# Order of expert-row gathers in a one-layer decoder kernel: value rows ahead of u rows, denser routing steps, one norm moved

## The chip, the cores and the metric

One core of a Trainium2 chip runs the kernel; the other cores are idle. The metric is device time in microseconds (us) for one execution of the whole layer. In the profile PE is TensorE (matmuls), PEld its weight loads, DVE is VectorE, ACT ScalarE, POOL GpSimd, SP SyncE. DMA transfers are issued from SP's queue (SPq), apart from the indirect gathers, which POOL issues.

## The reference, cut to what matters

1024 tokens of width 1024 pass through one decoder layer. The change concerns the last of its sublayers, PEER: each token picks 8 x 16 = 128 of 16384 single-neuron experts (product keys, two top-16 lists per head), and expert e adds g_e v_e gelu(u_e . x).

```python
x   = layer_norm(DN_ALPHA * x + mix, ln1_g, ln1_b)
ple = sigmoid(x @ ple_gate_w) * (p @ ple_proj_w)
ffn = peer(x, peer_wq, peer_subkeys, peer_u, peer_v)
x   = layer_norm(DN_ALPHA * x + ffn + ple, ln2_g, ln2_b)

# peer, for a block of 128 tokens: xb (t, d), ib and gb (t, 128)
u   = jnp.take(u_tab, ib, axis=0)                       # 128 rows of 1024 per token
hid = gelu(einsum("td,ted->te", xb, u))
vv  = jnp.take(v_tab, ib, axis=0)
out = einsum("te,ted->td", gb * hid, vv)
```

## The kernel before, in words

**Tiles and halves.** The 1024 tokens are eight tiles of 128. They go through the mixer and the projections in two halves of four tiles. `post(hf, ...)` takes a half from the mixer's output to the end of the embedding: output projection, first layer norm, queries and scores of eight heads, then the per-layer embedding (four blocks of the gate and projection matmuls). The second half's `post(1, m)` carries the writing of dense gates in its embedding: `dense_gates` (L961 to L990) of two tiles, whose steps stand between the embedding's matmuls.

**Two ways to the experts.** Four tiles, GT = (0, 1, 6, 7), here gathered blocks 0 to 3, fetch their experts' rows. Four, DT = (4, 5, 2, 3), go through all 16384 experts as dense matmuls with a gate matrix that is zero where an expert wasn't picked. The dense part, `dense` (from L992), is the last stage: `hidden` (L1026) computes 128 experts' activations (matmuls named ph), `value` (L1046) multiplies by the value table (matmuls pv) and adds into acc (L1059). At its end the generator of gathers is drained, the two row vectors of the second layer norm are loaded (`norm2`, L951) and four norms are done (`finish`, L1082).

**The gathers.** For a gathered block, `gather_u` (L838) has 128 steps: one indirect DMA on POOL (L844) brings one u row for each of the 128 tokens (a tile of 128 x 1024 float32), and one DVE instruction (L846) multiplies it with x and accumulates. `gather_v` (L854) has 32 rounds: four indirect DMAs (L873), then eight matmuls (L880, 16 records in the trace) that add the four rows' contributions into the PSUM tile ffn. Behind the last round it takes the norm's row vectors (norm2), bt, the statistics and the norm.
The rows of both live in one ring of ROWS = 7 buffers in order of emission, with MORE = 4 more in the dense part. `route` (L741) turns a tile's scores into expert numbers and gates in 29 or 30 steps, nearly all on DVE: 16 selections (`select16`, L730, on the tile sc), eight of the candidates, one of ranks, four of key lookups, and for a gathered tile the transposed index list.

**The order.** `gathers` weaves three generators, us (u rows), routes and vs (value rows): `weave` (L901) takes one step of each in turn, and a step that can't go on yet yields -1. `pump` (L230) runs this generator from within the main work: each matmul group gives credits (at RATE 0.8, 0.6, 1.0, 1.2 by phase), and each step costs its yield (1.46 a row, 0.7 to 2.0 a route step). Phase 2 is `post(1, m)`, phase 3 the dense part. Steps emitted in phase 3 have priority over the dense work (LATER is -10000), and are held (PIN, issue_after) behind the last DVE instruction ahead of the dense part. Value rows of a block need all of its u rows; routes start only when the tile's half is scored (flow["scored"]), and block 3's route only when block 0 is done.

Of the kernel before, what the change touches and what calls it, by code (L numbers as in the profile page):

```python
# [14 lines left out]
ALU = mybir.AluOpType  # L15
# [9 lines left out]
NH = T // HT  # L25
TT = HT // P
# [10 lines left out]
GT = (0, 1, 6, 7)  # L37
DT = (4, 5, 2, 3)
# [29 lines left out]
def kernel(ctx: ExitStack, tc: tile.TileContext, a: dict, out: bass.AP, tap=None):  # L68
    nc = tc.nc
# [65 lines left out]
    def row_bcast(t, src):  # L135
        nc.sync.dma_start(t, bass.AP(tensor=src.tensor, offset=src.offset, ap=[[0, P], [1, D]]))
        return t
# [82 lines left out]
    flow = {"it": None, "credit": 0.0, "rate": 0.0, "scored": 0, "phase": 0, "routing": False}  # L220
# [30 lines left out]
    def row(name):  # L251

        flow["rows"] = flow.get("rows", -1) + 1
        pool = more[0] if more and flow["rows"] % (ROWS + MORE) >= ROWS else gath
        return pool.tile([P, D], F32, name=name, tag="rows")
# [341 lines left out]
    def layer_norm(y, st, g, b, w):  # L597

        mv = small.tile([P, 2], F32, name=f"mv{w}")
        nc.vector.bn_aggr(mv, st)  # L600
        rs = small.tile([P, 1], F32, name=f"rs{w}")
        nc.scalar.activation(rs, mv[:, 1:2], AF.Sqrt, bias=eps_l)
        nc.vector.reciprocal(rs, rs)
        nc.vector.scalar_tensor_tensor(y, y, mv[:, 0:1], g, op0=ALU.subtract, op1=ALU.mult)
        nc.vector.scalar_tensor_tensor(y, y, rs, b, op0=ALU.mult, op1=ALU.add)
# [120 lines left out]
    def drain(it):  # L726
        for _ in it:
            pass

    def select16(v, i, n, s):  # L730
# [5 lines left out]
        nc.vector.max_index(i[:, n, 8:16], v[:, n, 8:16], s)  # L736

    def route(ti, dense, R, lists=None):

        if dense:  # L740
# [97 lines left out]
    def gather_u(ti, idx, idxT, gate, H):  # L838
        x1 = peer.tile([P, D], F32, name="x1g")
        nc.sync.dma_start(x1, x1_d[ti])  # L840
        hid = small.tile([P, NSEL], F32, name="hid")
        for s in range(NSEL):
            ug = row("ug")
            nc.gpsimd.indirect_dma_start(out=ug, out_offset=None, in_=a["peer_u"],  # L844
                                         in_offset=bass.IndirectOffsetOnAxis(ap=idx[:, s:s + 1], axis=0))
            nc.vector.scalar_tensor_tensor(ug, ug, 1.0, x1, op0=ALU.mult, op1=ALU.mult, accum_out=hid[:, s:s + 1])  # L846
            yield 1.46
        if tap:
            tap(f"hid{ti}", hid)
        nc.scalar.activation(hid, hid, AF.Gelu)  # L850
        nc.vector.tensor_mul(hid, hid, gate)
        H.append(hid)

    def gather_v(ti, idx, idxT, gate, H):  # L854
        ffn = ps_f.tile([P, D], F32, name="ffn")
        nc.tensor.transpose(ffn[:, :P], H[0], ident)
        pw = small.tile([P, P], F32, name="pw")
        nc.scalar.activation(pw, ffn[:, :P], AF.Copy)
        N = 4
        for ph in range(32 // N):  # L860

            w32 = peer.tile([P, 4, N, 32], F32, name="w32", bufs=2)
            nc.gpsimd.memset(w32, 0.0)
            for c in range(4):
                dst = w32[:, c].rearrange("p r e -> p (r e)")[:, ph * N:ph * N + (N - 1) * 33 + 1:33]
                nc.scalar.activation(dst, pw[:, 32 * c + ph * N:32 * c + ph * N + N], AF.Copy)
            for r in range(N):

                rows_v = []
                for c in range(4):  # L870
                    t = 32 * c + ph * N + r
                    vg = row("vg")
                    nc.gpsimd.indirect_dma_start(out=vg, out_offset=None, in_=a["peer_v"],  # L873
                                                 in_offset=bass.IndirectOffsetOnAxis(ap=idxT[:, t:t + 1], axis=0))
                    rows_v.append(vg)
                    if c < 3:
                        yield 1.46
                with ExitStack() as side:
                    for n, (e, c) in enumerate((e, c) for e in range(2) for c in (3, 0, 1, 2)):
                        mm = nc.tensor.matmul(ffn[32 * c:32 * c + 32, e * 512:(e + 1) * 512], w32[:, c, r],  # L880
                                              rows_v[c][:, e * 512:(e + 1) * 512], start=ph == 0 and r == 0,
                                              stop=ph == 32 // N - 1 and r == N - 1, skip_group_check=True)
                        if n == 0:

                            side.enter_context(tc.issue_after(mm.ins))
                            side.enter_context(tc.high_priority())
                yield 1.46
        ln2 = norm2()
        bt = row("bt")
        st = small.tile([P, 2, 6], F32, name="st2")  # L890
        nc.sync.dma_start(bt, base_d[ti])
        for e in range(2):
            es = slice(e * 512, (e + 1) * 512)
            nc.vector.scalar_tensor_tensor(bt[:, es], bt[:, es], 0.5, ffn[:, es], op0=ALU.mult, op1=ALU.add)
            nc.vector.bn_stats(st[:, e], bt[:, es])
        finish(ti, bt, st, ln2)

    def weave(*its):

        its = list(its)  # L900
        while its:  # L901
            stuck = True
            for it in list(its):
                x = next(it, None)
                if x is None:
                    its.remove(it)
                elif x >= 0:
                    yield x
                if x is None or x >= 0:
                    stuck = False  # L910
            if stuck:
                yield -1.0

    def gathers():

        H = {t: [] for t in GT}
        done = []

        def routes():
            while at[0] < ROUTE:  # L920
                yield -1.0
            for t in sorted((t for t in range(T // P) if t % TT >= DIRECT[t // TT]), key=lambda t: (t // TT, t in GT)):

                while t in GT and GT.index(t) > 2 and len(done) < GT.index(t) - 2:
                    yield -1.0
                while flow["scored"] <= t // TT:
                    yield -1.0
                flow["routing"] = True
                yield from route(t, t in DT, R)
                flow["routing"] = False  # L930

        at = [0]

        def us():
            for t in GT:
                while t not in R:
                    yield -1.0
                for x in gather_u(t, *R[t], H[t]):
                    at[0] += 1
                    yield x  # L940

        def vs():
            for t in GT:
                while not H[t]:
                    yield -1.0
                yield from gather_v(t, *R[t], H[t])
                done.append(t)

        yield from weave(us(), routes(), vs())

    def norm2():  # L951

        return [row_bcast(row(n), a[n]) for n in ("ln2_g", "ln2_b")]

    def finish(ti, bt, st, ln2):
        layer_norm(bt, st, *ln2, 2)
        nc.sync.dma_start(out[ti * P:(ti + 1) * P], bt)
# [35 lines left out]
    def dense(X):  # L993
        with ExitStack() as dctx:
# [7 lines left out]
            st = [a_p.tile([P, 2, 6], F32, name=f"std{c}") for c in range(TT)]  # L1002
# [74 lines left out]
                W = Wn  # L1077
            if flow["it"] is not None:
                drain(flow["it"])
            ln2 = norm2()  # L1080
            for c in range(TT):
                finish(DT[c], acc[c], st[c], ln2)  # L1082

    R = {}

# [39 lines left out]
    for n in range(2):  # L1125
        nc.sync.dma_start(X[n][:, :, ND * P:].bitcast(F32), xs_d[n])
    flow["rate"], flow["phase"] = RATE[3], 3
    dense(X)


# [54 lines left out]
```

## Time and profile before

| | us |
|---|---|
| median of 3 runs | 3281.31 (3279.74 to 3281.79) |
| profiled execution | 3276.95 |
| its span | 3275.1 |
| its mean granted TensorE clock | 0.958 of full |

| engine | busy us | share of the span |
|---|---|---|
| PE | 3043.4 | 93% |
| PEld | 2320.7 | 71% |
| DVE | 2338.4 | 71% |
| ACT | 1197.7 | 37% |
| POOL | 1177.0 | 36% |

The profile moves 954.45 MB, 291 GB/s on average; the gathers are 536.94 MB of it. Busy times overlap between engines, and a share over the whole span is a mean over stages: the mixers, the second half's `post` with its embedding (about 1400 to 1573 us), the dense part (to about 3232 us) and what follows it. The span stands 1.85 us below the time of its execution.

### The profile page before, as it was taken

Reading aid. Unit: us, or ns where it says so; the run is one execution under the profiler, and the core shown is the slowest. Engines: PE = TensorE matmul, PEld = TensorE weight load, DVE = VectorE, ACT = ScalarE, POOL = GpSimd, SP = SyncE. Lnnn points to the kernel's source line nnn. Section 1 sums busy time; section 2 is a strip of 40 time slices with the busy share of each in tenths; the row PEclk is TensorE's granted clock in tenths of the full one; section 3 lists DMA queues with packets and bytes.
Section 4 is the critical chain, followed back from the end, with each engine's and each line's share of the span. In section 5 each row is a group of like instructions: output and inputs, shape, how many; then the busy total and the mean of one; then the engine's idle time right before and its main releaser. Section 6 shows DMA issues by size and latency. Waiting matters only on the chain.

```text
span 3275.1 us, 48259 instructions
## 1 busy us (share of the span) xinstructions
PE 3043.4 (93%) x17160; PEld 2320.7 (71%) x17160; DVE 2338.4 (71%) x5615; ACT 1197.7 (37%) x2258; POOL 1177.0 (36%) x1066
## 2 busy tenths in 40 slices
PE   8999989787899898877899999999999999999996
PEld 6778777666777686667677777777777777777663
DVE  7656557977789799997888866666676666665333
ACT  6433323262344365566423322222233222223220
POOL 0000000434422345351344544444544445443453
PEclk9999999898999998888999999999999999999997
DMA  4444355787777898998999999999988999998998
GB/s 169 143 169 152 135 186 169 281 301 267 295 274 247 298 357 310 337 313 273 320 346 345 339 330 326 340 335 350 329 325 322 344 334 334 341 328 316 354 320 303
DMA packets 368914, 954.45 MB, mean 291 GB/s; under 512 B 34432, under 2 KB 116480, under 8 KB 364576
## 3 DMA queue, kind: packets, MB, share of 16 engines
q0 software_dynamic: 147456, 536.94, 44.9%
q1 hardware_dynamic: 221216, 414.43, 36.1%
q8 instruction: 135, 2.21, 0.3%
q14 instruction: 107, 0.88, 0.1%
HBM read 862.10 MB, written 89.13 MB: 290 GB/s over the span
## 4 chain that ended last, share of the span: by engine, by line
PE 73%; DVE 13%; DMA 5%; ACT 4%; issue 3%; POOL 1%; SPq 0%; DVEq 0%; POOLq 0%; ACTq 0%
PE ph L263 7%; PE ffn L880 7%; PE ph L265 7%; PE pv L263 7%; PE pv L264 7%; PE ph L264 7%; PE pv L265 7%; DVE ug L846 3%; DMA vg<-in_peer_v_dram,idxT 1%; PE pg L985 1%; DMA ug<-in_peer_u_dram,idx 1%; PE pgr L263 1%; PE pgr L264 1%; PE pgr L265 1%; PE pgb L265 1%
## 5 line engine op out<-in xcount | busy, mean ns | idle before, releaser
L844 POOL DMA_INDIRECT ug<-in_peer_u_dram,idx x512 | 602.9, 1178 | 1417.2 <-DVE idxT L831 598.4
L873 POOL DMA_INDIRECT vg<-in_peer_v_dram,idxT x512 | 555.6, 1085 | 650.0 <-DVE ug L846 291.2
L846 DVE SCALAR_TENSOR_TENSOR ug<-ug,x1g 128x1024 f32<-128x1024 f32 x512 | 619.6, 1219 | 37.6 <-DMA ug<-in_peer_u_dram,idx 35.2
L263 PE MATMUL ph<-x1hl,uh 128*128 128x512 f32 x1024 | 408.4, 399 | 9.7 <-ACT uh L259 9.7
L265 PE MATMUL ph<-x1hl,ul 128*128 128x512 f32 x1024 | 407.3, 398 | 2.2 <-DVE ul L260 2.2
L264 PE MATMUL ph<-x1hl,uh 128*128 128x512 f32 x1024 | 407.5, 398 | 0.0
L264 PE MATMUL pv<-vl,wdh 128*128 128x512 f32 x1024 | 402.9, 394 | 0.0
L265 PE MATMUL pv<-vh,wdl 128*128 128x512 f32 x1024 | 399.9, 392 | 0.0
L263 PE MATMUL pv<-vh,wdh 128*128 128x512 f32 x1024 | 398.0, 394 | 0.0
L259 ACT ACTIVATE uh<-ur 128x512 fp32r<-128x512 f32 x256 | 159.8, 626 | 445.6 <-PE ph L264 430.5
L880 PE MATMUL ffn<-vg,w 128*32 128x512 f32 x2048 | 272.8, 620 | 27.8 <-DMA vg<-in_peer_v_dram,idxT 27.7
L259 ACT ACTIVATE vh<-vr 128x512 fp32r<-128x512 f32 x256 | 160.8, 628 | 359.3 <-PE pv L265 341.1
L260 DVE TENSOR_TENSOR ul<-ur,uh 128x512 fp32r<-128x512 f32 x256 | 175.7, 688 | 153.1 <-ACT uh L259 150.0
L1059 DVE SCALAR_TENSOR_TENSOR acc<-acc,pv 128x512 f32<-128x512 f32 x256 | 167.6, 682 | 129.8 <-PE pv L265 129.7
L260 DVE TENSOR_TENSOR vl<-vr,vh 128x512 fp32r<-128x512 f32 x256 | 176.0, 687 | 111.0 <-ACT vh L259 110.7
L263 PEld LDWEIGHTS ph<-x1hl,uh 128*128 128x128 f32 x1024 | 193.0, 188 | 72.1 <-issue 15.1
L263 PEld LDWEIGHTS pv<-vh,wdh 128*128 128x128 f32 x1024 | 192.1, 188 | 62.4 <-issue 21.0
L264 PEld LDWEIGHTS pv<-vl,wdh 128*128 128x128 f32 x1024 | 192.3, 188 | 61.5 <-issue 19.3
L265 PEld LDWEIGHTS ph<-x1hl,ul 128*128 128x128 f32 x1024 | 192.8, 188 | 59.6 <-issue 9.2
L264 PEld LDWEIGHTS ph<-x1hl,uh 128*128 128x128 f32 x1024 | 192.9, 188 | 55.4 <-issue 10.9
L265 PEld LDWEIGHTS pv<-vh,wdl 128*128 128x128 f32 x1024 | 192.3, 188 | 54.4 <-issue 12.6
L985 PE MATMUL pg<-oi,oj 128*128 128x128 f32 x1024 | 157.9, 297 | 39.0 <-ACT oi L984 15.6
(477 smaller groups left out, 5967.0 us busy)
## 6 DMA issues: line engine op xcount, KB each, us to landing
ur<-in_uT_dram SPq DMA_DIRECT2D x256, 256.0 KB, 6.3
vr<-in_peer_v_dram SPq DMA_DIRECT2D x256, 256.0 KB, 6.5
g_d<-gst SPq DMA_DIRECT2D x32, 1024.0 KB, 12.7
gt<-g_d SPq DMA_DIRECT2D x32, 1024.0 KB, 8.9
raw_zx<-in_w_z_dram SPq DMA_DIRECT2D x16, 512.0 KB, 5.8
raw_zv<-in_w_v_dram SPq DMA_DIRECT2D x16, 512.0 KB, 6.2
raw_zy<-in_w_z_dram SPq DMA_DIRECT2D x16, 512.0 KB, 4.5
raw_ga<-in_w_z_dram SPq DMA_DIRECT2D x16, 512.0 KB, 5.3
```

Of the source, the lines that this page charges most:

```text
L259: nc.scalar.activation(h, src, AF.Copy)
L260: nc.vector.tensor_tensor(l, src, h, op=ALU.subtract)
L263: nc.tensor.matmul(o, wh, xh, start=first, stop=False)
L264: nc.tensor.matmul(o, wh, xl, start=False, stop=False)
L265: nc.tensor.matmul(o, wl, xh, start=False, stop=last)
L844: nc.gpsimd.indirect_dma_start(out=ug, out_offset=None, in_=a["peer_u"], in_offset=bass.IndirectOffsetOnAxis(ap=idx[:, s:s + 1], axis=0))
L846: nc.vector.scalar_tensor_tensor(ug, ug, 1.0, x1, op0=ALU.mult, op1=ALU.mult, accum_out=hid[:, s:s + 1])
L873: nc.gpsimd.indirect_dma_start(out=vg, out_offset=None, in_=a["peer_v"], in_offset=bass.IndirectOffsetOnAxis(ap=idxT[:, t:t + 1], axis=0))
L880: mm = nc.tensor.matmul(ffn[32 * c:32 * c + 32, e * 512:(e + 1) * 512], w32[:, c, r], rows_v[c][:, e * 512:(e + 1) * 512], start=ph == 0 a ...
L985: nc.tensor.matmul(o[:, :, r], oj[:, t], oi, start=True, stop=True)
L1059: nc.vector.scalar_tensor_tensor(acc[c][:, es], acc[c][:, es], 0.5 if g == 0 else 1.0, o[c], op0=ALU.mult, op1=ALU.add)
```

## The change

Three things are altered.

1. In the second half's embedding (phase 2, both halves scored; the new function `embedding`), `weave` no longer takes one step of each generator in turn. It goes through them from the last to the first, vs, routes, us, and stops at the first that gives a step. `routes` doesn't begin a tile there. A route that has already begun goes on only when vs has no step.
2. In the dense part (phase 3) `routes` passes on only every third step of a route, so three of its steps go in one turn of the weave.
3. For the last gathered block, `gather_v` no longer issues its final sum, statistics and norm behind its last round: it loads its norm rows and bt there, and leaves the rest as a function `end` in the list `ends`. The dense part's end takes those same norm rows instead of loading its own pair, does its four norms, and then calls `end`.

```diff
         bt = row("bt")
         st = small.tile([P, 2, 6], F32, name="st2")
         nc.sync.dma_start(bt, base_d[ti])
-        for e in range(2):
-            es = slice(e * 512, (e + 1) * 512)
-            nc.vector.scalar_tensor_tensor(bt[:, es], bt[:, es], 0.5, ffn[:, es], op0=ALU.mult, op1=ALU.add)
-            nc.vector.bn_stats(st[:, e], bt[:, es])
-        finish(ti, bt, st, ln2)
+
+        def end():
+            for e in range(2):
+                es = slice(e * 512, (e + 1) * 512)
+                nc.vector.scalar_tensor_tensor(bt[:, es], bt[:, es], 0.5, ffn[:, es], op0=ALU.mult, op1=ALU.add)
+                nc.vector.bn_stats(st[:, e], bt[:, es])
+            finish(ti, bt, st, ln2)
+
+        if ti == GT[-1]:
+            ends.append((end, ln2))
+        else:
+            end()
+
+    ends = []
+
+    def embedding():
+        return flow["phase"] == 2 and flow["scored"] == NH
 
     def weave(*its):
         its = list(its)
         while its:
             stuck = True
-            for it in list(its):
+            last = embedding()
+            for it in reversed(its) if last else list(its):
                 x = next(it, None)
                 if x is None:
                     its.remove(it)
@@ -908,6 +922,8 @@
                     yield x
                 if x is None or x >= 0:
                     stuck = False
+                    if last:
+                        break
             if stuck:
                 yield -1.0
 
@@ -923,10 +939,13 @@
-                while flow["scored"] <= t // TT:
+                while flow["scored"] <= t // TT or embedding():
                     yield -1.0
                 flow["routing"] = True
-                yield from route(t, t in DT, R)
+                for n, x in enumerate(route(t, t in DT, R)):
+                    if flow["phase"] < 3 or n % 3 == 2:
+                        yield x
                 flow["routing"] = False
 
@@ -1077,9 +1096,10 @@
             if flow["it"] is not None:
                 drain(flow["it"])
-            ln2 = norm2()
+            end, ln2 = ends.pop()
             for c in range(TT):
                 finish(DT[c], acc[c], st[c], ln2)
+            end()
```

## Rows read from the trace of the kernel before

**Rows 1.** Windows by stage: length, busy us (records) per engine, PEclk, DMA share, GB/s.

```profile
core 0: us, PE busy (x) PEld busy (x) DVE busy (x) ACT busy (x) POOL busy (x), PEclk, DMA share, GB/s
1400.00:1573.00 173.00, 131.88 (x950) 117.75 (x950) 148.68 (x360) 117.50 (x337) 61.90 (x46) 0.88 0.88 290
1573.00:1800.00 227.00, 224.82 (x1037) 166.12 (x1038) 190.69 (x578) 76.25 (x139) 100.80 (x90) 0.98 0.93 342
1800.00:2999.00 1199.00, 1199.00 (x5592) 879.53 (x5591) 809.81 (x1421) 353.05 (x647) 569.23 (x529) 1.00 0.91 335
...
3232.00:3275.00 43.00, 14.11 (x76) 2.31 (x68) 17.62 (x28) 1.36 (x5) 9.36 (x10) 0.60 0.70 274
```

**Rows 2.** DVE instructions by line, 1400 to 1573: busy us, mean ns, idle before.

```profile
L976 DVE TENSOR_TENSOR one<-iota,Tb 128x1024 bf16<-128x1024 bf16 x32 | 39.0, 1219 | 17.4 <-ACT Tb L968 13.6 <-ACT oi L984 3.8
L978 DVE TENSOR_TENSOR oj<-iota,Tb 128x1024 f32<-128x1024 bf16 x32 | 39.0, 1217 | 0.3 <-PE pg L985 0.2
L846 DVE SCALAR_TENSOR_TENSOR ug<-ug,x1g 128x1024 f32<-128x1024 f32 x23 | 27.7, 1216 | 2.1 <-DMA ug<-in_peer_u_dram,idx 2.0
```

**Rows 3.** Windows of the u rows' tile ug: DVE and POOL busy us (records).

```profile
0.00:1400.00 1400.00, 229.38 (x379) 236.94 (x192) 0.93 0.69 241
1400.00:1573.00 173.00, 27.41 (x46) 32.37 (x22) 0.88 0.88 290
...
1800.00:2999.00 1199.00, 312.91 (x513) 282.61 (x255) 1.00 0.91 335
```

**Rows 4.** Windows of the value rows' tile vg: PE, PEld, POOL.

```profile
0.00:1400.00 1400.00, 33.75 (x240) 6.81 (x240) 77.74 (x64) 0.93 0.69 241
1400.00:1573.00 173.00, 9.85 (x80) 2.20 (x80) 28.44 (x22) 0.88 0.88 290
...
1800.00:2999.00 1199.00, 135.63 (x1024) 28.11 (x1024) 277.96 (x258) 1.00 0.91 335
```

**Rows 5.** Timeline of POOL, end of the embedding: start, length, instruction, idle before.

```profile
1515.77 0.94 POOL L844 DMA_INDIRECT ug<-in_peer_u_dram,idx  x1 [0.31 <-PE pg L985]
...
1561.30 1.68 POOL L873 DMA_INDIRECT vg<-in_peer_v_dram,idxT  x1 [44.05 <-DVE ug L846]
```

**Rows 6.** Timeline of PE around one round of value rows in the dense part.

```profile
2018.79 0.39 PE L265 MATMUL pv<-vh,wdl 128*128 128x512 f32 x1
2019.02 0.40 PE L263 MATMUL ph<-x1hl,uh 128*128 128x512 f32 x1
2019.35 1.93 PE L880 MATMUL ffn<-vg,w 128*32 128x512 f32 x16
2021.20 0.50 PE L263 MATMUL pv<-vh,wdh 128*128 128x512 f32 x1
```

**Rows 7.** Timeline of the end, from the last dense accumulate on.

```profile
3232.36 0.67 DVE L1059 SCALAR_TENSOR_TENSOR acc<-acc,pv 128x512 f32<-128x512 f32 x1
...
3239.70 3.64 PE L880 MATMUL ffn<-vg,w 128*32 128x512 f32 x16 [1.02 <-DMA vg<-in_peer_v_dram,idxT]
...
3248.86 0.33 SPq L136 DMA_DIRECT2D ln_g<-in_ln_g_dram  x1
...
3252.41 3.64 PE L880 MATMUL ffn<-vg,w 128*32 128x512 f32 x16 [3.54 <-DMA vg<-in_peer_v_dram,idxT]
...
3270.30 1.28 DVE L605 SCALAR_TENSOR_TENSOR acc<-acc,rs,ln_b 128x1024 f32<-128x1024 f32 x1
```

**Rows 8.** Windows of the score tile sc: DVE busy us (records).

```profile
1400.00:1573.00 173.00, 17.67 (x108) 0.88 0.88 290
1573.00:1800.00 227.00, 24.30 (x148) 0.98 0.93 342
```

**Rows 9.** Timeline of POOL where u rows run alone.

```profile
622.75 1.51 POOL L844 DMA_INDIRECT ug<-in_peer_u_dram,idx  x1 [0.30 <-issue]
624.57 1.09 POOL L844 DMA_INDIRECT ug<-in_peer_u_dram,idx  x1 [0.30 <-issue]
```

**Rows 10.** Timeline of PE at a wait for ul in the dense part.

```profile
1598.75 0.79 PE L265 MATMUL ph<-x1hl,ul 128*128 128x512 f32 x1 [2.18 <-DVE ul L260]
```

## The prediction for the changed kernel

> **What bounds the kernel now.** I read the stages first [rows 1]. From 1573 us on, in the dense part, TensorE (PE) is busy without a gap at a granted clock of 0.98 to 1.00 of full, that is at its upper level of 2.4 GHz, until the last dense matmul at about 3232 us. Ahead of it, in the second half's embedding (1400 to 1573 us), PE is busy 131.9 of 173 us at a mean clock of 0.88, while VectorE (DVE) is busy 148.7 us, so there DVE is the fullest engine. Behind the dense part, 3232 to 3275, PE has only five rounds of gathered value rows left and waits for their rows.
>
> The second view counts the gathers. One u row costs DVE 1.216 us [rows 2]; with two DVE records a row, 379 + 46 records [rows 3] are 212 rows by 1573 us. One round of value rows is four gathers and 16 matmul records; 240 + 80 records [rows 4] are 20 rounds, 80 v rows. The credits in the code agree: the embedding pumps 17 gate blocks x 4 x 0.9 + 4 x (4 x 2.64 + 4 x 0.66) = 114 credits at rate 1.0, a turn of one u, one route step and one v costs 1.46 + 1.0 + 1.46, so 29 turns. By them u stands at 208 and v at 80 at its end.
>
> The third view is GpSimd's queue (POOL) at the stage's end: its last gathers go out at 1516 us and the next only at 1561.30, after 44 us in which it waited for a u row's DVE instruction [rows 5]. The rows in the ring were u rows that the dense part's steps had already fetched, and their DVE work is held behind the last embedding instruction (issue_after). So the gathers run out of credit there, not of bandwidth.
>
> **Value rows first.** With only v turns, 114 / 1.46 = 78 turns fit: 77 v rows instead of 29, and one u instead of 29. Counted from where the last head is scored (u 180, v 51), the first gathered block (block 0, tile GT[0]) would be finished at 128 v rows; u stands at 181 instead of 208; route 6 (29 of its 30 steps lay here) goes to the dense part. So at most 48 v rows, 12 rounds, move ahead of the dense part. What a round takes from PE there: between the dense matmuls around one, 2019.02 to 2021.20 is 2.18 us where two neighbours stand 0.23 apart [rows 6], so about 2.0 us. Twelve are 24 us. The lower bound is the ring: by the code only 7 rows exist before the dense part (11 in it), and a round holds four of them, so with 7 rows hardly more than one round is in flight. If a round in the embedding takes as long as two of those at the end (2 x 6.35 us, from 3239.70 to 3252.41 for two, [rows 7]), 160 us hold 13 rounds instead of 19, so 6 of the 12 are left over. I take 8 rounds: 16 us less (range 8 to 24).
>
> In the embedding itself DVE loses 27 x 1.216 = 33 us of u rows and 17.67 us of score selection [rows 2, 8], some 50 of its 148.7 us. What is late next: PE gets 12 x 2.0 us on top of 131.9, 156 of 173 us; the DMA engines are 88% busy already. So the stage can't shrink by the 50; the bounds are 0 and PE's and DMA's rest, some 25 us. I take 12 us less, nearer to nothing since the gate pairs (39 + 39 us, [rows 2]) and the write of the gates stay in one chain.
>
> **Three route steps a turn, and where the DVE work goes.** The 33 us of u rows and route 6 come back at the head of the dense part. A route costs 24.30 us of selection over 16 steps [rows 8], in a window that holds all of route 7 and a few steps of 6, and about as much again for the rest; the part of route 6 that lay before 1573 us is some 18 us. So about 50 us more DVE work lands between the start of the dense part and the end of the u rows of the second gathered block (block 1, tile GT[1]). Before, the same stretch (1573 to 1800) leaves 227 - 190.7 = 36 us of DVE idle [rows 1]. The excess is 14 us; dense work takes DVE for somewhat under half of PE's time (DVE 809.8 of 1199 us with 313 us of u rows in it, [rows 1, 3]: 0.41), so 14 us of it cost PE about 14 / 0.41 = 34 us, less the 12 us by which DVE may start ahead of PE's first dense matmul (PE waits there today). I take +25 us. Bounds: 0, if the u rows are spread, and some 110, worked out under the rival below. That three steps go in one turn adds no work; it puts the route's instructions ahead of u rows in the order and saves two thirds of its credits. Credits do not bind in the dense part: by the code all steps are issued by about two thirds of it, while the trace still has v rows at its end [rows 7]. I cost it at nothing; it hides behind the selection's own chain of loads.
>
> Steady gathers go at 1199 us / (257 u + 256 v) = 2.34 us each [rows 3, 4]. That pace doesn't change.
>
> **The last norm.** After the last dense accumulate at 3232.36 the chain is: five rounds to 3256, then bt's sum, statistics and norm, with the four dense norms in between and behind, the last instruction at 3270.30 and the end at 3275 [rows 7]. The change takes away one pair of row loads (issued at 3248.86, in the shadow of the last round) and puts the four dense norms (two DVE passes of 1.28 us each, as the last instruction is one) ahead. If the gathers still end last, the dense norms lie beside the rounds and what follows the last round falls from 19 (3256 to 3275) to about 10 us: 9 us less. If the dense part ends last, some 18 to 20 us follow 3232 instead of 43. Twelve rounds fewer and the free POOL time before 1561 bring the gathers some 25 us forward, so I take the second: 23 us less (range 5 to 25).
>
> **The sum**, on the profiled 3276.95 us: -12 - 16 + 25 - 23 = -26, 3251. That execution lies 4.4 us under the median of 3281.3, so the forecast is 3256 us.
>
> A caveat from the Trainium skill on the 16 us: "Perfetto Trace Analysis", Identifying the Most-Contended Engine, holds that matmul busy time is no measure of how full PE is, and "TensorE: Matmul & The Clock Gate" (its section on the 56 ns gap) gives 215.7 ns between warm 512-column matmuls. By rows the spacing is 0.23 us, some 6% above that page's. If that rest were room that could be used, a round moved away would bring nothing, and by this the forecast would be 3272; nothing in the rows shows the room in use.
>
> **The rivals.** *DVE too full at the start of the dense part* (slower). The dense part's steps have priority over dense work, and now there are no v rows in the ring to space the u rows: block 1 still has 75 of them. Where u rows ran alone, they came 1.8 us apart [rows 9]; 75 take 135 us, in which they hold DVE for 75 x 1.216 = 91 us; routes 6 and 7 take perhaps 40% of the rest. DVE's share for dense work is then close to nothing, and PE, which needs 0.41 of it, loses up to 110 us. For it: at 1598 us PE stood 2.18 us for a ul behind route steps [rows 10]; against it: such waits stayed short there, and PE's input rings hold three tiles. It decides from a loss of about 51 us on, where the -26 turns to nothing; at 80 us the time is 3256 + 55 = 3311.
>
> *The gathers become the end.* v rows of block 1 can't start before its 75 u rows are done; if those are slowed by DVE to 3 us or more, all later rows shift by as much as the embedding gave, and the end stays with the last rounds. Then only the 9 us of the norm are left against a few us of delay: 3279, no change.
>
> *All of it comes.* All 12 rounds fit, the embedding gives 25 us, the dense part starts without a stall: -25 - 24 + 0 - 23, 3209; with a little stall 3215.
>
> *It doesn't do what it says*: with 7 rows the v rows go no faster alone than before beside u rows, and the u rows and route are only put off: 3276.
>
> **How the numbers follow.** Forecast 0.38 (3236 to 3274), DVE too full 0.26 (3288 to 3345), gathers last 0.14, all of it 0.14 (3200 to 3235), not done 0.08. A measurement of this kernel tells about 0.2% from no change, 6.6 us. Faster: 0.36 + 0.14 + 0.03 = 0.53; within: 0.02 + 0.08 + 0.05 + 0.02 = 0.17; slower 0.30. The range leaves out the lower part of "all of it" and the upper part of "DVE too full": 3222 to 3318.
>
> **What would show it.** In the changed profile: v matmul records before the first dense matmul (320 now; up to 512), and 27 fewer u rows; the first dense matmul at about 1560; DVE busy share and PE idle in the first 230 us of the dense part (PE idle over 50 us there is the first rival); the last v round before or after the last dense accumulate; 18 to 20 us from that accumulate to the end. The forecast is wrong if PE waits for ul or vl for long at the dense start, or if the last rounds still lie alone at the end.

## The result and the profile after

| | before | after |
|---|---|---|
| median, us | 3280.5 | 3325.9 |
| profiled execution, its span | 3276.95, 3275.1 | 3329.47, 3327.7 |
| first dense matmul | 1572.9 | 1572.6 |
| last dense accumulate | 3232.4 | 3223.1 |
| last round of value rows starts | 3252.4 | 3312.3 |
| rounds ahead of, in and behind the dense part | 20, 104, 4 | 29, 82.5, 16.5 |

The change makes the kernel slower: the ratio after to before, with its 95% interval, is 1.0151 (1.0133 to 1.0169). The medians above by themselves give 1.0138, 45 us, and the two profiled spans lie 52.6 us apart. The forecast was 3256 and the range ended at 3318; the time lies above it.

The windows by stage of the kernel after, with the columns of [rows 1]:

```profile
1400.00:1573.00 173.00, 142.25 (x1079) 115.74 (x1071) 101.19 (x164) 123.02 (x358) 62.61 (x54) 0.92 0.93 307
1573.00:1800.00 227.00, 193.24 (x787) 147.75 (x786) 190.30 (x447) 61.78 (x104) 110.96 (x85) 0.92 0.91 336
1800.00:2999.00 1199.00, 1199.00 (x5561) 889.47 (x5560) 835.89 (x1680) 357.79 (x657) 526.90 (x492) 1.00 0.87 317
2999.00:3232.00 233.00, 228.97 (x1148) 154.40 (x1146) 116.81 (x204) 62.00 (x123) 111.85 (x115) 0.99 0.90 326
3232.00:3328.00 96.00, 42.41 (x240) 7.93 (x240) 15.17 (x20) 1.87 (x11) 49.80 (x54) 0.72 0.89 341
```

Read them beside [rows 1]. In the embedding DVE lost 47.5 us of work (148.68 to 101.19) and the first dense matmul comes when it came before. At the head of the dense part PE is idle 227 - 193.24 = 33.8 us, where it was 2.2. And behind the dense part, from 3232 us on, lie 240 matmul records, 15 rounds, where there were four or five. The last two make up the sum. The dense part, from its first matmul to its last accumulate, is 8.9 us shorter (1659.4 to 1650.6): 31.6 us more idle PE, and 1320 records of rounds in it for 1660, 21 rounds fewer. What lies behind that accumulate grew from 42.8 to 104.6 us, by 61.8. So -0.3 - 8.9 + 61.8 = 52.6, the whole difference. The last round lay behind the dense part in the kernel before too; now **the gathers end 60 us later**, and the dense part, which ends 9 us sooner, isn't what sets the time.

Why they are late stands in POOL's queue. Its timeline in the kernel after, at its two longest gaps (start, length, instruction, idle before and what ended it):

```profile
1766.44 1.15 POOL L844 DMA_INDIRECT ug<-in_peer_u_dram,idx  x1 [2.01 <-DVE ug L846]
1839.51 0.94 POOL L844 DMA_INDIRECT ug<-in_peer_u_dram,idx  x1 [71.91 <-DVE idx L827]
...
1884.33 0.94 POOL L873 DMA_INDIRECT vg<-in_peer_v_dram,idxT  x1 [4.19 <-DVE v L732]
1961.91 0.94 POOL L873 DMA_INDIRECT vg<-in_peer_v_dram,idxT  x1 [76.65 <-PE ffn L880]
```

For 71.9 us, and after a short burst for another 76.7, no gather goes out. In the trace no gather overtakes a waiting one, so whatever stands behind it in POOL's queue waits too. **The first standstill**: block 1's u rows are all fetched by 1767, and the next in the queue is block 2's first u row, whose expert numbers (idx, L827) come from route 6, which ends only at 1839. **The second**: block 1's value rows fill the ring, and PE's first round for them doesn't come. The timelines of PE and DVE around it, and then of PE in the kernel before:

```profile
1843.44 0.27 PE L829 MATMUL pidx<-ident,idf 128*128 128x128 f32 x1
...
1948.74 0.27 PE L829 MATMUL pidx<-ident,idf 128*128 128x128 f32 x1
1949.53 0.28 DVE L831 CAST idxT<-pidx 128x128 int32<-128x128 f32 x1
1954.18 0.27 PE L856 MATMUL ffn<-ident,hid 128*128 128x128 f32 x1
```

```profile
1821.37 0.27 PE L829 MATMUL pidx<-ident,idf 128*128 128x128 f32 x1
...
1830.11 0.27 PE L856 MATMUL ffn<-ident,hid 128*128 128x128 f32 x1
...
2414.71 0.27 PE L829 MATMUL pidx<-ident,idf 128*128 128x128 f32 x1
```

The tile ffn of a block and the tile pidx, through which a route transposes its index list, share one PSUM buffer (the pool ps_f has bufs=1, both tiles the tag "ffn"), and take it in the order in which the generators emitted them. In the changed kernel that order is pidx of block 2 (1843), pidx of block 3 (1949), ffn of block 1 (1954). So block 1's first round waits for the end of block 3's route. In the kernel before, the order was pidx of block 2 at 1821.37, ffn of block 1 at 1830.11, and pidx of block 3 behind all of block 1, at 2414.71. The two orders differ for one reason: block 3's route may begin when block 0 has given out its last value row, and value rows first bring that forward, ahead of the end of block 1's u rows and so of block 1's first value row.

What it costs: by 1962 us the kernel before has issued 455 gathers (291 u and 164 value rows), the changed one 407 (267 and 140), 48 fewer. At the end 264 matmul records stand behind the last dense accumulate for 68, 12.25 rounds or 49 rows more. There, with no dense work beside them, rounds follow each other in (3312.32 - 3232.37) / 14 = 5.7 us, 1.43 us a row. So 12.25 rounds take 70 us; less the 6 us that the moved norm gives (e1 below) that is 64, about the 62 found. At the pace of 2.34 us in the dense part 49 rows would have taken 115 us; the rows come faster once the dense part is over.

The end of the kernel after, with the first and the last of those rounds:

```profile
3232.37 1.92 PE L880 MATMUL ffn<-vg,w 128*32 128x512 f32 x16 [1.56 <-DMA vg<-in_peer_v_dram,idxT]
...
3312.32 3.61 PE L880 MATMUL ffn<-vg,w 128*32 128x512 f32 x16 [2.98 <-DMA vg<-in_peer_v_dram,idxT]
...
3322.75 1.29 DVE L605 SCALAR_TENSOR_TENSOR bt<-bt,rs,ln_b 128x1024 f32<-128x1024 f32 x1
```

### The profile page after: what moved, and what is told of

Same layout as the page of the kernel before. It is cut to its first block, busy times and chain, and to the rows that moved or that the text cites. A ratio compares the mean times of both kernels' runs of the same rounds, so it can differ in the third digit from the quotient of the medians.

```text
span 3327.7 us, 48244 instructions
## 1 busy us (share of the span) xinstructions
PE 3056.1 (92%) x17160; PEld 2326.7 (70%) x17160; DVE 2340.1 (70%) x5615; ACT 1198.3 (36%) x2258; POOL 1176.9 (35%) x1066
## 4 chain that ended last, share of the span: by engine, by line
PE 54%; DMA 7%; DVE 6%; ACT 2%; issue 2%; POOL 1%; SPq 0%; POOLq 0%; DVEq 0%; ACTq 0%
PE ffn L880 7%; PE ph L265 7%; PE ph L263 7%; PE ph L264 7%; PE pv L263 7%; PE pv L264 7%; PE pv L265 7%; DMA vg<-in_peer_v_dram,idxT 3%; DVE ug L846 2%; PE pg L1004 2%; DMA g_d<-gst 1%; DMA ur<-in_uT_dram 1%; ACT oi L1003 1%; DMA vr<-in_peer_v_dram 1%; POOL vg L873 1%
## 5 line engine op out<-in xcount | busy, mean ns | idle before, releaser
L263 PE MATMUL pv<-vh,wdh 128*128 128x512 f32 x1024 | 385.5, 395 | 6.7 <-DVE acc L1078 5.7
L880 PE MATMUL ffn<-vg,w 128*32 128x512 f32 x2048 | 280.9, 646 | 57.3 <-DMA vg<-in_peer_v_dram,idxT 57.1
L880 PEld LDWEIGHTS ffn<-vg,w 128*32 128x32 f32 x2048 | 57.6, 113 | 203.7 <-issue 135.8
```

Source lines behind the costliest of these rows:

```text
L263: nc.tensor.matmul(o, wh, xh, start=first, stop=False)
```

## The experiments

Two theories stood at first. The *standstill theory*: the loss is the two gaps of POOL. The *full-DVE theory*, the first rival of the prediction: the loss is PE's 34 us of idle time at the dense start. The kernel before ran beside each group; its median lay between 3276 and 3289 us, so ratios are compared, with their 95% interval.

| kernel | ratio to before | interval | PE idle, first 230 us of the dense part | last dense accumulate, last matmul of a round |
|---|---|---|---|---|
| after | 1.0151 | 1.0133 to 1.0169 | 33.8 | 3223, 3315 |
| e1 norm last alone | 0.9984 | 0.9969 to 1.0000 | 1.8 | 3230, 3254 |
| e2 one route step | 1.0158 | 1.0131 to 1.0185 | 30.9 | 3223, 3313 |
| e3 old order | 0.9983 | 0.9966 to 1.0000 | 4.0 | 3237, 3261 |
| e4 route 7 late | 1.0056 | 1.0032 to 1.0081 | 32.4 | 3247, 3276 |
| e5 only its transpose late | 1.0059 | 1.0036 to 1.0082 | 32.7 | 3248, 3277 |
| e6 both repairs | 1.0005 | 0.9991 to 1.0018 | 25.9 | 3256, 3245 |
| e12 both, short u rows | 0.9944 | 0.9929 to 0.9960 | 13.3 | 3246, 3240 |

**e1, the norm alone.** The kernel before, with `end`, `ends` and the new end of `dense` from the diff, nothing else.

> The kernel before with part 3 of the change alone (last gathered block's norm behind the four dense norms, one pair of row loads less). Standstill theory (the changed kernel's loss comes from two stretches, 72 and 77 us long, in which no gather goes out): none of this is in here, and the gathers still end last, so the 9 us of the forecast for that case: about 3272 us. Full-DVE theory (the loss is PE waiting for VectorE at the start of the dense part): the same 3272. If the part costs something by itself, over 3281.

3271.3 against 3277.6, ratio 0.9984: 5 us faster, at the limit of what can be told. From the last round to the end of the span it was 20.1 us before (3255.0, the last matmul's start, to 3275.1) and is 14.1 here (3254.1 to 3268.2). So the part gives 5 to 7 us where the gathers end last, for the 9 of the forecast.

**e2, one route step a turn.**

```diff
-                    if flow["phase"] < 3 or n % 3 == 2:
-                        yield x
+                    yield x
```

> The changed kernel with one route step a turn in the dense part. Standstill theory: both routes are still given out within 60 turns, ahead of block 1's 75 u rows, so the index transpose of block 3 stays ahead of block 1's ffn in the one PSUM tile and the second standstill (77 us) stays; the first one may change by some 20 us either way: 3310 to 3345. Full-DVE theory: route work is spread over three times the u rows, PE idle at the dense start falls from 33 us to under 20: about 3305 or less.

1.0158: as slow as the change. The two standstills are there, 71.9 and 73.8 us long. The full-DVE theory expected 3305 or less here. How many steps of a route go in a turn makes no difference here, in either direction; PE's idle time is 30.9, so spreading the steps doesn't relieve DVE either. The step of the prediction that cost this part at nothing holds.

**e3, the old order in the embedding.** Three steps a turn and the last norm stay.

```diff
-            last = embedding()
+            last = False
...
-                while flow["scored"] <= t // TT or embedding():
+                while flow["scored"] <= t // TT:
```

> The changed kernel without its first part: one step of each generator in turn in the embedding too, routes allowed there; three route steps a turn and the last norm stay. Both theories put the loss on the order of the embedding: u stands at 208 at the dense start, no standstill over 20 us, about 3270 us, as the last norm alone. If three route steps a turn are what does the harm (the third standpoint), the time stays over 3300.

0.9983, the same as the norm alone. All of the loss, some 1.7%, comes with the embedding's order.

**e4, the last block's route late.**

```diff
-                while t in GT and GT.index(t) > 2 and len(done) < GT.index(t) - 2:
+                while t in GT and GT.index(t) > 2 and len(begun) < GT.index(t) - 1:
...
+                begun.append(t)
                 yield from gather_v(t, *R[t], H[t])
```

> The changed kernel, with the route of the last gathered block begun only when block 1's value rows have begun, so that its index transpose takes the one PSUM tile behind block 1's ffn. Standstill theory: the second standstill (77 us) goes, the first (72 us) stays, the gathers end some 50 to 77 us sooner: 3250 to 3280. Full-DVE theory: PE idle at the dense start stays near 33 us and with it most of the loss: 3310 to 3325.

1.0056: 31 us of the loss are gone, and PE idle 32.4 us as before. POOL's waits between 1560 and 1990 us in e4 (who waited for whom, us in total, times, longest):

```profile
POOL ug L844 <- DVE idx L827: 72.0, 1, 72.0
POOL ug L844 <- PE ffn L880: 36.6, 5, 23.1
...
POOL vg L873 <- PE ffn L880: 14.5, 5, 3.9
```

The second standstill has gone and the first has stayed, as the theory said. Full DVE can't explain this step: its sign was PE's idle time, and that didn't move. The gain is less than 77 us, because the value rows that no longer lie at the end lie in the dense part (94 rounds for 82.5) and it ends 23 us later.

**e5, only the transpose late.** The route itself runs where it ran in the change; the transpose waits.

```diff
+        while ti == GT[-1] and len(flow["begun"]) < 2:
+            yield -1.0
         o = ps_f.tile([P, D], F32, name="pidx", tag="ffn")
```

> The changed kernel; the route of the last gathered block runs where it ran, but holds its index transpose back until block 1's value rows have begun. PSUM theory (the second standstill comes from the one PSUM tile, which the transpose takes ahead of block 1's ffn): the same as with the whole route held back, 3285 to 3305. Route-work theory (what stands in the way is that route's work on VectorE and its loads): the standstill stays, 3315 to 3330.

1.0059, the same as e4 within the intervals. It isn't that route's work on DVE, nor its loads, but its place in the queue for the one PSUM buffer.

**e6, both repairs.** To e4's edit, the embedding gives route steps beside value rows, still without u rows, so that block 2's route is done in time.

```diff
             for it in reversed(its) if last else list(its):
+                if last and not stuck and it is its[0]:
+                    break
                 x = next(it, None)
...
-                    if last:
-                        break
...
-                while flow["scored"] <= t // TT or embedding():
+                while flow["scored"] <= t // TT:
```

> The changed kernel with both repairs: the last gathered block's route begun late, as before, and in the embedding route steps alternate with value rows (still no u rows there), so that block 2's route is done at the dense start. Standstill theory: no standstill of over 20 us is left, the gathers come some 20 to 30 us sooner than with the first repair alone: 3255 to 3275. If value rows first cost by themselves (block 1's 75 u rows alone at the dense start hold VectorE): PE idle of some 30 us at the dense start stays and the time is 3285 to 3300.

1.0005: no change to before, and no standstill (POOL's longest wait between 1560 and 1990 is 11.8 us). The last round is over by 3246, ahead of the last dense accumulate at 3256: **the dense part is the end**, and with it PE's idle time comes into the count, 25.9 us. Where it lies in e6:

```profile
1573.00:1700.00 127.00, 120.98 (x527) 87.78 (x528) 111.08 (x309) 39.27 (x65) 53.12 (x49) 0.97 0.96 357
1700.00:1800.00 100.00, 82.51 (x317) 62.90 (x316) 99.76 (x243) 26.53 (x52) 59.31 (x47) 0.91 0.93 331
```

From 1700 to 1800, where 45 u rows follow one another with no round of value rows between them, DVE is busy 99.76 us, PE 82.5, and the granted clock falls to 0.91. The time fits neither range of the expectation: it is just above the first, but the sign of the second, PE's idle time, stayed. Both theories hold, one behind the other: the standstills hide the full DVE.

**e7, e10, e11, more credit with the old order.** e3 with credits of the second half at 1.3, 1.1 and 1.2.

```diff
-RATE = (0.8, 0.6, 1.0, 1.2)
+RATE = (0.8, 0.6, 1.3, 1.2)
```

> The changed kernel without its first part (the order before in the embedding), with credits in the second half at rate 1.3 for 1.0, so that the gathers don't run out of credit there. Credit theory (44 us of idle POOL at the embedding's end are for want of credit): some 10 to 19 more gathers lie ahead of the dense part, 3245 to 3265. If VectorE or the row ring limits them there: no change, 3270, or some us slower for later gates.

> The changed kernel without its first part, credits in the second half at rate 1.1. At 1.0 the gathers' last round ended some 24 us behind the last dense accumulate, at 1.3 some 20 us ahead of it, while that accumulate came 14 us later. If the two ends trade evenly, both meet between: dense end about 3240, last round about 3250, time 3262 to 3268. If later gates in the embedding eat what the gathers gain: 3272.

> The same with rate 1.2. If the two ends trade evenly: dense end about 3246, last round about 3241, and 18 us behind the dense end: 3262 to 3268. If not, 3272 as at 1.0 and 1.3.

Ratios 1.0000 (0.9986 to 1.0013), 1.0025 (1.0015 to 1.0036) and 1.0033 (1.0020 to 1.0045). At 1.3 there were indeed 92 value rows and 220 u rows ahead of the dense part for 80 and 212, and the last round lay 20 us ahead of the dense end; but that part began at 1582 (1576 in e3) and ended at 3251. At 1.1 and 1.2 it began at 1605 and 1608 (on a chip where the kernel before took some 12 us longer), and the ends don't trade evenly. What the gathers gain, the later start of the dense part takes back. At 1.3 it isn't the gates that are late: their last matmul (tile pg) comes at 1576.2, for 1586.1 in e3. The first dense matmul waits for its first tile of the u table (ur), which SP's queue gives out at 1573.7, for 1569.1 in e3. At 1.1 and 1.2 that load goes out at 1592.6 and 1593.9, behind the last write of the gates (1587.9 and 1592.9). Why it stands there isn't settled.

**e8, both repairs with credit at 1.3.** e6 and the edit of e7.

> Both repairs, with credits in the second half at rate 1.3. Standstill theory with credits as the limit: a few more rounds ahead of the dense part than with both repairs, 3240 to 3265. If the ring of 7 rows limits value rows in the embedding (waits for the matmuls of a round were 99 us there in the changed kernel): no more rounds than with both repairs, the same time.

1.0085 (1.0062 to 1.0108), slower than either outcome expected. 116 value rows for e6's 109 ahead of the dense part, which starts at 1588.6 for 1569.9, with PE idle for 35.4 us at its head. POOL's waits for the rounds' matmuls, from 1400 to 2100 us, were 170.9 us, so the ring held the value rows up. As in e7, the dense start waits for ur and not for the gates: ACT stood 12.0 us for that load, and the last gate matmul came at 1575.0.

**e9, short u rows in the change.** To see whether DVE or the transfers starve PE, and make route 6 late, the u rows of block 1 from the 54th on are multiplied over 256 of their columns. The other 768 are left out of the sum, so this is a probe and not a version to use.

```diff
-            nc.vector.scalar_tensor_tensor(ug, ug, 1.0, x1, ..., accum_out=hid[:, s:s + 1])
+            n = 256 if ti == GT[1] and s >= 53 else D
+            nc.vector.scalar_tensor_tensor(ug[:, :n], ug[:, :n], 1.0, x1[:, :n], ..., accum_out=hid[:, s:s + 1])
```

> The changed kernel; the u rows of block 1 from the 54th on, those that lie in the dense part, are multiplied over 256 of their 1024 columns only (768 are left out of the sum), so that each holds VectorE for some 0.4 us instead of 1.22; their transfers stay as they are. Full-DVE theory (PE's 34 us of idle time at the dense start and the late route of block 2 both come from VectorE, which 75 u rows in a row fill): PE idle there falls under 12 us and the first standstill, 72 us, under 40; about 3280 to 3310. Transfer theory (u rows in a row crowd out the dense part's own loads): PE idle stays at 25 to 45 us, the time at 3310 or over.

1.0039 (1.0025 to 1.0054). The first standstill fell from 71.9 to 13.8 us, which was DVE's doing: route 6 had stood between u rows there. POOL's waits in e9 between 1560 and 1990 us:

```profile
POOL vg L874 <- PE ffn L881: 111.7, 7, 75.6
...
POOL ug L844 <- DVE idx L827: 13.8, 1, 13.8
```

The second stays at 75.6, since nothing was done to the PSUM order. PE's idle time fell to 23.8 us only, not under 12, so not all of it hangs on the length of the u rows' DVE work.

**e12, short u rows with both repairs.** The same edit on e6, from the 59th row on, where nothing else stands in the way.

> Both repairs, and the u rows of block 1 from the 59th on, those in the dense part, are multiplied over 256 of their 1024 columns only (768 are left out of the sum). With both repairs alone no standstill was left, and PE still lost 26 us in the first 230 us of the dense part, 17 of them between 1700 and 1800 us, where VectorE was busy 99.8 of 100 us. Full-DVE theory: that loss falls under 12 us and the dense part ends 14 to 25 us sooner, a ratio of 0.992 to 0.996 to the kernel before. Transfer theory: the loss stays near 26 us, ratio 1.000.

0.9944 (0.9929 to 0.9960): 0.6% better than e6, some 20 us. PE is idle 13.3 us for 25.9, and the dense part is 18 us shorter (1686.4 to 1668.1 us from first matmul to last accumulate). The stretch that was full in e6, here:

```profile
1700.00:1800.00 100.00, 92.01 (x379) 71.10 (x378) 72.53 (x246) 31.43 (x62) 49.61 (x49) 0.98 0.99 373
```

DVE falls from 99.76 to 72.53 us and PE gains 9.5. Half of PE's idle time was DVE's doing; some 13 us stay with DVE no longer full and the transfers at 0.99, and what they are isn't settled.

**e13, the embedding without gathers.** Open was why the first dense matmul stayed where it was when DVE lost 47 us.

```diff
-        if flow["it"] is None:
+        if flow["it"] is None or flow["phase"] == 2 and flow["scored"] == NH:
             return
```

> The changed kernel with no step of the gathers given out in the second half's embedding (their work moves to the dense part). Chain theory (the gate steps one, oi, pg, gst and their write set the stage's length): the dense part's first matmul comes at about 1570 us as before and after the change, within 5 us. Sharing theory (what PE and the transfers do for value rows, or VectorE for u rows, holds the stage): it comes 12 us or more sooner, at 1560 or before. The whole is slower either way, 3350 to 3400 us: some 60 gathers more, at 1.3 us each where they run alone at the end, on top of the changed kernel's time, less what PE gives back.

The first dense matmul of e13,

```profile
1514.32 0.50 PE L263 MATMUL ph<-x1hl,uh 128*128 128x512 f32 x1 [1.11 <-ACT uh L259]
```

comes 58 us sooner than in the change, so by the sign that was set the chain theory fell. But that sign misleads: in e13 this matmul isn't the embedding's end. The gates' matmuls (tile pg) of the kernel before, the change and e13, each with its first and last start from 1350 us on:

```profile
L985 PE MATMUL pg<-oi,oj x584: 270/275/583, 1349.8 to 1583.0; 128*128 128x128 f32 x195
L1004 PE MATMUL pg<-oi,oj x586: 270/275/582, 1350.1 to 1571.1; 128*128 128x128 f32 x196
L1004 PE MATMUL pg<-oi,oj x610: 270/275/580, 1351.4 to 1567.8; 128*128 128x128 f32 x153
```

With no gathers in the stage, 96 dense matmuls came forward in between the gates' last ones; in the change there are none, in the kernel before 18. Behind the last gate PE then stood idle up to the first matmul of the value table:

```profile
1585.90 0.79 PE L263 MATMUL pv<-vh,wdh 128*128 128x512 f32 x1 [17.85 <-ACT wdh L259]
```

So the gates end only 3 us sooner than in the change. In e13 the last score matmul (tile psc), ahead of the stage, starts later, at 1366.4 for 1357.5 us; counted from there the gates take 201.4 us for 213.6. Sixteen rounds less (13 for 29) give 12 us, 0.8 us a round, and the first matmul of the value table comes 24 us sooner by the same count (219.5 for 243.3 us), 1.5 us a round. In the dense part 21.25 fewer rounds took 40.5 us (8.9 + 31.6), 1.9 us a round. So no run shows a round to be dearer in the embedding than in the dense part, and without the rounds the gates still take 201 of 214 us, which is nearer to the chain theory than its sign was. The measure is rough: route steps and dense matmuls came forward into the stage too. By the ratio, 1.0133 (1.0100 to 1.0166, two executions), the whole is about as slow as the change, for the rows come at the end instead; the expectation, 3350 or more, was too high.

## Why the prediction was wrong

- **The embedding, -12.** Measured, at the first dense matmul: -0.3. The relief of DVE did what was forecast to the gates: their last matmul moved from 1583.0 to 1571.1 us, by 11.9. The step that failed is to take the end of the gates for the start of the dense part. Before, 18 dense matmuls had run ahead of the last gate matmul; in the change all of them stand behind it, so the start stays where it was. Why they no longer go in between isn't shown.
- **Rounds moved ahead, -16 for eight.** Nine rounds moved, 20 to 29, so the count, and the ring as its limit, was right: 200 records in 173 us are 12.5 rounds, 13.8 us each, for the 12.7 taken from [rows 7]; POOL waited 99.0 us for the rounds' matmuls there. Their price in the dense part agrees as well, 1.9 us for 2.0 [rows 6], by a sum that doesn't separate the lower granted clock at the head of the changed kernel's dense part (0.92 for 0.98). The caveat by the Trainium skill ("Perfetto Trace Analysis", Identifying the Most-Contended Engine), by which such a round might have brought nothing, isn't borne out: taking rounds away shortened the dense part by about their rows' length. What the step left out is that 12.25 more rounds left the dense part for its far end, where they cost 5.7 us each.
- **DVE at the dense start, +25.** Measured: 31.6 us of PE idle time. Size and mechanism were about right, as e6 and e12 show (half of the idle time in e6 was DVE's doing), and so was the rival's picture of u rows alone: 138 records, 69 rows, in the 194 us to 1767, with DVE busy 50.00 of 50 us from 1650 and 99.97 of 100 from 1700. The rival's bound of 110 was far off: in the 117 us from 1650 to 1767 DVE was busy throughout, and PE still for 92 of them. In the changed kernel PE's idle time costs nothing by itself, since the gathers end last; what the full DVE does cost there is the late route 6, as e9 shows. PE's idle time decides only once the standstills are mended.
- **The tail, -23.** Measured: +61.8, and this is the step that failed most. I let "twelve rounds fewer and the free POOL time" bring the gathers 25 us forward and counted only how many rows stood where; the last round came 60 us later. I never asked what each block's first row waits for once the order changes. The put-off route 6 was costed as DVE work (18 us), not as the thing that block 2's u rows, and everything behind them in POOL's queue, wait for (71.9 us). And that pidx shares one PSUM buffer with ffn is in the code, and no step of the prediction looked at it (76.7 us).
- **The rivals.** "The gathers become the end" had the right end, and said that block 1's value rows would start late. It looked for the delay in slow u rows of 3 us or more. They came 2.8 us apart (69 rows in the 194 us, for 37 rows before), and the last of block 1 was fetched at 1766.4 us, for 1778.6 before; the delay came after them. It was priced at "a few us" against the norm's 9, 3279, where the two standstills made it 3326. The range's upper end, 3318, came from the full-DVE rival, whose mechanism is there and isn't the bound.
- **Two slips in the sum.** 34 us less 12 is 22, where 25 was taken, and 3281.3 less 26 is 3255, where 3256 stands. Nothing hangs on either.
- **What would show it.** Value records ahead of the first dense matmul: 464 (said: 320 up to 512); u rows 32 fewer (27); the first dense matmul at 1572.6 (1560); the last rounds alone at the end, which was named as the sign of a wrong forecast. PE's idle time in the first 230 us, 33.8, stayed under the 50 named for the first rival.

Apart from e12, which leaves part of the sums out, no version tried is clearly faster than the kernel before; the norm moved to the end, alone or with three route steps, is about 0.2% faster, with intervals that end at 1.0000.

## What to carry to other kernels

When the order of woven generators changes, follow each shared buffer and each in-order queue in the new order of emission: who takes the buffer next, and what the head of the queue waits for. A row count ahead of a stage says nothing of the rows behind it. And take a stage's end from its own last instruction: the first one of the next stage can stay where it is while the stage gets 12 us shorter, as in the change, or come forward by 58 us while the stage ends 3 us sooner, as in e13.

## What was not expected of the hardware

Gathers with no dense work beside them run at 1.43 us a row at the end of the changed kernel, against 2.34 beside the dense part, so what is late by many rows is caught up in part.

In e6, from 1700 to 1800 us, DVE was busy 99.76 us, PE stood idle for 17.5 us, and the granted clock was 0.91; in the kernel before PE was busy through that stretch at 1.00. In e12, with DVE at 72.53 us, PE was idle 8.0 us there and the granted clock was 0.98. Over the whole dense part e12 has 11.7 us less of idle PE than e6 and is 18.3 us shorter, with as many rounds in it. By an estimate from these numbers, some 6 us of what the full DVE costs lie in time in which PE is busy; that all of it is the clock isn't shown.
